# Dilated attention by pairs of heads, with queries and keys stored by class

## The chip, the cores and the metric

The kernel runs on one core of a Trainium2 chip. The time is device microseconds from the first to the last instruction of that core, with what lies around it; the median of the runs counts. Before the change it is 3844.45 us (three runs, 3839.64 to 3844.83).

## What is computed

Two models follow each other on 512 tokens of 1024 features. The first block (two layers: convolution with an mLSTM, then latent attention) is the same before and after the change. The second block has two layers too; each projects the normed tokens to queries, keys and values for two kinds of attention, mixes both by gates, and ends with a feed-forward network. The two kinds:

```python
def differential_attention(q, k, v, lam_full, subln_g, lambda_init):
    ...
        s = jnp.einsum('bqhcd,bkhcd->bhcqk', qblk, kk, ...) * scale
        p = jax.nn.softmax(s, axis=-1)
        a = p[:, :, 0] - lam_full * p[:, :, 1]
        return jnp.einsum('bhqk,bkhe->bqhe', a.astype(v.dtype), v)
...
for g, (window, dilation) in enumerate(((128, 1), (512, 4), (2048, 16))):
    qg = apply_rope(parts[base].reshape(B, S, DB_HEADS, DB_HEAD_DIM), cos, sin)
    kg = apply_rope(parts[base + 1].reshape(...), cos, sin)
    og, lg = dilated_window_attention(qg, kg, vg, dilation, (window // 2) // dilation)
    outs.append(og); lses.append(lg)
wts = jax.nn.softmax(jnp.stack(lses), axis=0)
ob = jnp.einsum('gbsh,gbshd->bshd', wts, jnp.stack(outs))
```

Differential attention has 4 heads of two parts with 64 features each. Dilated attention has 8 heads of 64 features and three groups: a window of 64 tokens to either side; every fourth token; every sixteenth token.

## The kernel before

Tokens are 512 columns, features lie on the 128 rows of a tile, so a tile of queries holds two heads: one on rows 0 to 63, the other on rows 64 to 127. A projection (`fm_g`, lines 365 and 366) adds up 24 products of 128 x 128 by 512 in one of four accumulators `ps_mm`; weights and inputs are in a high and a low part of type fp32r. These products are the "fills": `work()` in `mixer2` yields them a few at a time, and `fill` puts them between the steps of attention by hand-written amounts in us of TensorE (`FILL`, line 1763).

`rope` (line 1518) follows the projection of queries and keys: ScalarE copies the accumulator, four DMAs from ScalarE's queue swap the halves of 32 rows into a tile `rsw` (three buffers), VectorE multiplies by the cosines, GpSimd multiplies the swapped tile by the sines, and VectorE adds both (line 1528).

`diff_unit` (line 1803) makes one head's differential attention for 128 queries: for each of two parts a product over all 128 rows (L1814) and one over the 64 rows of that part (L1815) into one bank `ps_st`, a softmax, transposes (L1835), and the product with the values (L1841). Between the two parts it yields, and fills come in between.

`dil_unit` (line 1863) takes one head `c` of a pair `hp` and one of four classes of tokens (`b`, every fourth token, 128 queries). Its scores are six products for the windows (L1869: 64 rows, 32 columns, 64 to 256 keys) and two for the groups with larger dilation (L1871: 64 rows, 128 columns, 128 keys), all of type fp32 into one bank. Queries and keys are stored in the order of the tokens, so the class is read with a step of four elements:

```python
cv = [a[r0 : r0 + 64].rearrange("p (i b) -> p i b", b=4) for a in t]
...
pe(mm(s[:, P + P * g : 2 * P + P * g], cv[2 * g][:, :, b], cv[2 * g + 1][:, :, b], start=True, stop=True))
```

A softmax on VectorE and ScalarE follows, four transposes (L1885), a copy to `pT` (L1886), and after all eight units of a pair the products with the values (L1898 and L1905), which alternate between the two heads, that is, between output rows 0 to 63 and 64 to 127. Four banks `ps_st` and four buffers `p` serve both kinds of units.

`attend` (line 1767) runs the units by steps: scores of the next unit, fill, transposes of an earlier one, fill, products with the values. `ahead` says how many units are scored before the first is transposed (1 for differential, 2 for dilated units). `mark` and `LAG` let a fill overtake the attention by so many steps at most. What the source orders so is only the order of tracing: a scheduler moves instructions on each engine by its own estimate of times within these bounds, so the order that is built is shown below where it matters.

In the first block one tile `con` holds all constants, loaded by one DMA ahead of the first weights (line 580).

Of the kernel before, what the change touches and what calls it, by code (L numbers as in the profile page):

```python
# [19 lines left out]
P = 128  # L20
D = 1024
KD = 8
# [13 lines left out]
# ---------------------------------------------------------------- parameters  # L36
# [15 lines left out]
_off = 0  # L52
for _n, _w in (
    ("I", 128), ("J", 128), ("NI", 128), ("NJ", 128), ("sel", 8), ("mF", 128), ("mB", 128),
    ("mcos", 64), ("msin", 64),
):
    _CON[_n] = (_off, _w)
    _off += _w
NCON = _off


def _consts():
    con = np.zeros((P, NCON), np.float32)

    def put(n, a):
        o, w = _CON[n]
        con[:, o : o + w] = a
# [34 lines left out]
# windows of 128 keys by first token; the first one goes on from the end at the start  # L102
# [32 lines left out]
def host(inputs):  # L135
# [37 lines left out]
    a["con"] = _consts()  # L173
# [57 lines left out]
# ---------------------------------------------------------------- the program  # L231
class Prog:
# [8 lines left out]
    # -- small helpers  # L241
# [4 lines left out]
    def con(self, n):  # L246
        o, w = _CON[n]
        return self.con_t[:, o : o + w]
# [32 lines left out]
    def weights(self, src, n=WC, lo=None):  # L281
        """A chunk of weights: its two parts, which add up to it."""
# [10 lines left out]
    def split_g(self, hi, lo, src, scale=None, bias=None):  # L293
        """The high part; the function returned makes the low one."""
# [39 lines left out]
    def mm3(self, out, a, b, first, last):  # L334
        """out += a.T b; a and b are (high, low)."""
# [5 lines left out]
    def pe(self, ins):  # L341
        """Other work traced after this does not overtake it by more than LAG stages."""
# [25 lines left out]
    def fm_g(self, wts, rhs, segs, m=P, tag="mm", every=0):  # L368
        """Features on partitions. wts: one (hi, lo, column) per K tile; segs: token ranges. Yields every so many K tiles."""
# [32 lines left out]
    def tm(self, lhss, wts, n, tags=("mm",) * 2 + ("ml",) * 3 + ("st",)):  # L402
        """Tokens on partitions, one output per entry of lhss: (hi, lo) per K tile; wts: (hi, lo, column) per K tile."""
# [11 lines left out]
    def rstd(self, blocks, dim, eps, name, more=None):  # L415
        """(mean + eps) ** -0.5 by token on partitions; blocks, and more to be added to them: [128 features, 128 tokens]."""
# [22 lines left out]
    def over(self, cols, out, mat="I"):  # L439
        """out[:, tokens]: a column by token on partitions, over all partitions along tokens."""  # L440
# [6 lines left out]
    def add_sq(self, S, k, src, a, tile):  # L447
        """Squares of one of the KD tiles, added up in S: [sum, the last ones]; a: the first token."""
# [15 lines left out]
    def factor(self, S, a, b):  # L464
        """The norm's factor for tokens a .. b, over all partitions."""
# [24 lines left out]
    def ada_first(self, d, pool, mp):  # L490
        """Shift and scale of one tile for the first norm."""
# [22 lines left out]
    def ada(self, layer, ch):  # L514
        """Columns 512 ch .. 512 ch + 2047 of the modulation of one layer, into mod[layer], in 16 steps. The four blocks of columns come one below the other."""
# [33 lines left out]
    def fill(self, us):  # L549
        """Steps of other work, for so long on the tensor engine."""  # L550
# [14 lines left out]
    def side(self, n=1):  # L565
        """The next steps of the modulation that is still to be made, between other work."""
# [6 lines left out]
    def first(self):  # L573
        """The first norm, h = rms(x) * (1 + scale) + shift, in two parts, and the first products, as far as the modulation has come."""
# [3 lines left out]
        with tc.tile_pool(name="n0", bufs=2) as tp, tc.tile_pool(name="raw0", bufs=self.RAW0) as rp:  # L578
            self.load_x()
            nc.sync.dma_start(self.con_t, I["con"])  # L580
# [44 lines left out]
    def turn(self, layer, s, hs, acc, tile):  # L625
        """For a norm by parts of the tokens, which follows the updates of x."""
# [9 lines left out]
    def turn_loop(self, st, R, a, b):  # L636
        """h = rms(x) * (1 + scale) + shift, in two parts, for some tokens."""
# [15 lines left out]
    def staged(self, srcs, rhs, ctx=False, tag="mm"):  # L653
        """Features on partitions for up to three chunks of weights, the first part of the tokens first."""
# [25 lines left out]
    # -- layer 0: conformer and mLSTM  # L680
    SEG = [(TC, TA), (0, TC)]

    def mixer0(self, hs, made):
        nc, tc, I = self.nc, self.tc, self.I
        SEG = self.SEG
        with tc.tile_pool(name="m0a", bufs=1) as mp, tc.tile_pool(name="m0t", bufs=2) as tp:
# [3 lines left out]

            cw = mp.tile([P, 4 * CONVW], F32, name="cw")
# [3 lines left out]
            # the gates first: theirs is a long chain  # L695
# [87 lines left out]
    def conv_g(self, mp, j, hs, cw, made=None):  # L783
        """Depthwise over tokens; both ranges in one padded row: y[o] is centred on column o + 15."""
# [40 lines left out]
    def conv_norm(self, mp, accs, mix):  # L825
        """Layer norm and silu of the convolution's output, in two parts."""
# [56 lines left out]
    def gates0(self, mp, tp, G16):  # L883
        """Per direction, by token on partitions: g = log i - cumulative log f, its running maximum G, exp(-m)."""
# [25 lines left out]
        # features on partitions, in the order of each direction's scan  # L910
# [892 lines left out]
    def diff_unit(self, ap, h, qb, qk, va, lam, of, sub):  # L1803
# [6 lines left out]
        for c in range(2):  # L1810
# [11 lines left out]
            if c == 0:  # L1822
                yield
# [287 lines left out]
```

## Time and profile before

| | |
|---|---|
| median of three runs | 3844.45 us |
| lowest, highest | 3839.64, 3844.83 us |
| span of the profiled execution | 3842.6 us |
| TensorE busy | 3718.7 us, 97% |
| weight loads | 3036.5 us, 79% |
| VectorE busy | 2183.8 us, 57% |
| ScalarE busy | 1437.0 us, 37% |
| GpSimd busy | 541.1 us, 14% |

The profile is of one execution. TensorE is in order, and its matmuls overlap: the time that a product costs is read from the start of one to the start of the next in the timeline, not from its duration. A product of type fp32 stands as two records; a projection's product has one. "Waits" are the idle times of an engine, put down to what ended them.

### The profile page before, as it was taken

Reading aid. Unit: us, or ns where it says so; the run is one execution under the profiler, and the core shown is the slowest. Engines: PE = TensorE matmul, PEld = TensorE weight load, DVE = VectorE, ACT = ScalarE, POOL = GpSimd, SP = SyncE. Lnnn points to the kernel's source line nnn. Section 1 sums busy time; section 2 is a strip of 40 time slices with the busy share of each in tenths; the row PEclk is TensorE's granted clock in tenths of the full one; section 3 lists DMA queues with packets and bytes.
Section 4 is the critical chain, followed back from the end, with each engine's and each line's share of the span. In section 5 each row is a group of like instructions: output and inputs, shape, how many; then the busy total and the mean of one; then the engine's idle time right before and its main releaser. Section 6 shows DMA issues by size and latency. Waiting matters only on the chain. (4 is left out here: it accounts for less than half of the span.)

```text
span 3842.6 us, 50218 instructions
## 1 busy us (share of the span) xinstructions
PE 3718.7 (97%) x19848; PEld 3036.5 (79%) x19848; DVE 2183.8 (57%) x3583; ACT 1437.0 (37%) x2507; POOL 541.1 (14%) x528
## 2 busy tenths in 40 slices
PE   7889999999999999999999999999999999999998
PEld 5667877888876767888888778888887887888887
DVE  6976554444447676655665544545567555445545
ACT  4334332222236555333453333432235433333222
POOL 3540100000024211000311200300031111021001
PEclk9989999999999999999999999999999999999999
DMA  5123223332110011332333322223323332222332
GB/s 200 61 91 127 88 91 121 115 110 66 61 51 30 27 34 54 100 98 95 114 90 98 93 64 83 83 90 102 99 81 113 99 90 76 63 95 84 94 98 77
DMA packets 107245, 336.88 MB, mean 88 GB/s; under 512 B 14849, under 2 KB 19457, under 8 KB 106753
## 3 DMA queue, kind: packets, MB, share of 16 engines
q1 hardware_dynamic: 94720, 316.88, 25.7%
q10 hardware_dynamic: 12288, 16.79, 1.7%
q8 instruction: 156, 2.56, 0.3%
q14 instruction: 81, 0.66, 0.1%
HBM read 310.54 MB, written 2.10 MB: 81 GB/s over the span
## 5 line engine op out<-in xcount | busy, mean ns | idle before, releaser
L286 ACT CAST whi<-raw 128x1024 fp32r<-128x1024 f32 (+2 forms) x488 | 501.8, 1031 | 1146.0 <-PE ps_mm L366 702.4
L287 DVE TENSOR_TENSOR wlo<-raw,whi 128x1024 fp32r<-128x1024 f32 (+2 forms) x488 | 616.4, 1265 | 384.0 <-ACT whi L286 381.0
L366 PE MATMUL ps_mm<-h,whi 128*128 128x512 f32 (+2 forms) x2593 | 643.4, 355 | 20.7 <-ACT cth L794 10.3
L366 PE MATMUL ps_mm<-xg,whi 128*128 128x512 f32 (+1 forms) x1929 | 571.7, 378 | 8.2 <-DVE xg L301 6.8
L366 PEld LDWEIGHTS ps_mm<-h,whi 128*128 128x128 f32 (+1 forms) x2593 | 429.1, 189 | 109.2 <-issue 17.3
L366 PE MATMUL ps_mm<-hid,whi 128*128 128x512 f32 (+1 forms) x1805 | 469.5, 357 | 0.0
L366 PEld LDWEIGHTS ps_mm<-xg,whi 128*128 128x128 f32 x1929 | 357.0, 189 | 79.3 <-DVE xg L301 11.2
L366 PE MATMUL ps_mm<-h,wlo 128*128 128x512 f32 (+2 forms) x1298 | 394.9, 354 | 0.5 <-DVE wlo L287 0.5
L365 PE MATMUL ps_mm<-xg,whi 128*128 128x512 f32 (+1 forms) x1207 | 377.3, 392 | 2.8 <-DVE xg L301 2.8
L366 PE MATMUL ps_mm<-xg,wlo 128*128 128x512 f32 (+1 forms) x966 | 362.4, 378 | 0.5 <-DVE wlo L287 0.5
L366 PEld LDWEIGHTS ps_mm<-hid,whi 128*128 128x128 f32 x1805 | 310.2, 188 | 59.4 <-issue 6.7
L366 PE MATMUL ps_mm<-hid,wlo 128*128 128x512 f32 (+1 forms) x903 | 299.0, 356 | 0.0
L365 PEld LDWEIGHTS ps_mm<-xg,whi 128*128 128x128 f32 x1207 | 216.0, 190 | 52.7 <-issue 13.1
L366 PEld LDWEIGHTS ps_mm<-h,wlo 128*128 128x128 f32 (+1 forms) x1298 | 217.9, 189 | 36.2 <-DVE wlo L287 1.0
L365 PE MATMUL ps_mm<-xg,wlo 128*128 128x512 f32 (+1 forms) x602 | 228.9, 383 | 0.0
L366 PEld LDWEIGHTS ps_mm<-xg,wlo 128*128 128x128 f32 x966 | 182.6, 189 | 33.8 <-DVE wlo L287 1.0
L366 PEld LDWEIGHTS ps_mm<-hid,wlo 128*128 128x128 f32 x903 | 160.4, 188 | 24.8
L1527 POOL TENSOR_TENSOR rsw<-rsw,rope 128x512 f32<-128x512 f32 x64 | 105.9, 1656 | 482.1 <-DMA rsw<-qk 439.9
L1153 DVE SCALAR_TENSOR_TENSOR xl<-ps_mm,mod,xl 128x512 f32<-128x512 f32 (+1 forms) x102 | 73.0, 718 | 108.5 <-PE ps_mm L366 108.0
L365 PEld LDWEIGHTS ps_mm<-xg,wlo 128*128 128x128 f32 x602 | 113.8, 189 | 23.1 <-issue 1.4
L365 PE MATMUL ps_mm<-whi,xg 128*128 128x512 f32 x384 | 131.8, 413 | 0.0
L818 DVE SCALAR_TENSOR_TENSOR acc<-up,cw,acc 128x783 f32<-128x783 f32 x80 | 122.7, 1534 | 2.2
(569 smaller groups left out, 5973.0 us busy)
## 6 DMA issues: line engine op xcount, KB each, us to landing
raw<-in_fup SPq DMA_DIRECT2D x88, 512.0 KB, 3.5
raw<-in_sup SPq DMA_DIRECT2D x88, 512.0 KB, 3.5
raw<-in_ada SPq DMA_DIRECT2D x80, 512.0 KB, 3.6
raw<-in_l_qk SPq DMA_DIRECT2D x48, 512.0 KB, 3.5
raw<-in_fdn SPq DMA_DIRECT2D x32, 512.0 KB, 3.4
raw<-in_d_v SPq DMA_DIRECT2D x32, 512.0 KB, 3.8
rsw<-qk ACTq DMA_DIRECT2D x256, 64.0 KB, 2.0
raw<-in_d_gt SPq DMA_DIRECT2D x32, 512.0 KB, 3.5
```

Source lines behind the costliest of these rows:

```text
L286: self.nc.scalar.copy(h[:, :n], r[:, :n])
L287: (lo or self.nc.vector).tensor_tensor(l[:, :n], r[:, :n], h[:, :n].bitcast(F32), ALU.subtract)
L365: return self.nc.tensor.matmul(out, w, x, **k)
L366: return self.nc.tensor.matmul(out, w, x, **k)
L818: nc.vector.scalar_tensor_tensor(acc, u, s, acc, ALU.mult, ALU.add)
L1153: self.pin(nc.vector.scalar_tensor_tensor(xs, o[:, : b - a], self.m(layer, 5, d, int(a < TC)), xs, ALU.mult, ALU.add))
L1527: nc.gpsimd.tensor_tensor(sw, sw, self.SR, ALU.mult)
```

## The change

`dil_unit` now takes both heads of a pair for one class. Each score product of the head on rows 0 to 63 is followed in the source by the same product of the head on rows 64 to 127, into another bank; then two softmaxes, eight transposes. `rope` gets a second form for the dilated queries and keys other than the window's keys: its last addition writes them sorted by class, so that the products read them without a step; its copy of the accumulator then takes an `rsw` buffer (four instead of three). `ahead` is 1 instead of 2 with two heads a unit, and the fills are doubled, so there is as much fill for a head as before. `diff_unit` no longer yields between its two parts: both products over 128 rows, then both over 64 rows. `LAG` is 6 and 4 instead of 8. The constants are in two tiles; the second is loaded when the mixer of the first layer begins. Comments and texts of functions are gone, which moves line numbers.

```diff
-    LAG = (9, 8)
+    LAG = (9, 6, 4)
...
-            self.con_t = cp.tile([P, NCON], F32, name="con")
+            self.con_ts = [cp.tile([P, NCON[0]], F32, name="con"), None]
...
+            self.con_ts[1] = mp.tile([P, NCON[1]], F32, name="con0")
+            nc.sync.dma_start(self.con_ts[1], I["con0"])
...
-    def rope(self, ap, ps):
+    def rope(self, ap, ps, classes=False):
         out = self.tl(ap, [P, T], "qk", bufs=self.QK)
-        nc.scalar.copy(out, ps)
-        sw = self.tl(ap, [P, T], "rsw", bufs=3)
+        raw = self.tl(ap, [P, T], "rsw", bufs=4) if classes else out
+        nc.scalar.copy(raw, ps)
+        sw = self.tl(ap, [P, T], "rsw", bufs=4)
...
+        if classes:
+            o, r, w = (t.rearrange(f, b=4) for t, f in (
+                (out, "p (b i) -> p b i"), (raw, "p (i b) -> p b i"), (sw, "p (i b) -> p b i")
+            ))
+            nc.vector.tensor_tensor(o, r, w, ALU.add)
...
-    FILL = ((1.2, 3.7, 1.2, 1.2), (3.5, 2.2, 1.2), (2, 1.2, 0.7), (4, 12))
+    FILL = ((2.4, 3.7, 1.2), (7, 4.4, 2.4), (4, 2.4, 1.4), (4, 12))
...
-        for c in range(2):
-            s = self.ps("st")
-            s_.append(s)
+        for c, s in enumerate(s_):
+            pe(mm(s, q[:, c, sl], k[:, c], start=True, stop=False))
+        for c, s in enumerate(s_):
             r = slice(64 * c, 64 * c + 64)
-            pe(mm(s, q[:, c, sl], k[:, c], start=True, stop=False))
             pe(mm(s, q[r, c, sl], kl[r], start=False, stop=True))
...
-    def dil_unit(self, ap, hp, c, b, t, vs, dm, of, pTs):
+    def dil_unit(self, ap, hp, b, t, vs, dm, of, pTs):
+        ss = [self.ps("st") for _ in range(2)]
+        rows = [slice(64 * c, 64 * c + 64) for c in range(2)]
+        cls = [a.rearrange("p (b i) -> p b i", b=4)[:, b] for a in t]
         for w in range(4):
...
+                for s, r in zip(ss, rows):
+                    pe(mm(
+                        s[32 * w : 32 * w + 32, c0 : c0 + n], cls[0][r, 32 * w : 32 * w + 32], t[1][r, t0 : t0 + n],
+                        start=True, stop=True,
+                    ))
         for g in (1, 2):
-            pe(mm(s[:, P + P * g : 2 * P + P * g], cv[2 * g][:, :, b], cv[2 * g + 1][:, :, b], start=True, stop=True))
+            for s, r in zip(ss, rows):
+                pe(mm(s[:, P + P * g : 2 * P + P * g], cls[2 * g][r], cls[2 * g + 1][r], start=True, stop=True))
```

What the scheduler makes of it on TensorE in the dilated stage. A row is line, operation, output and inputs; `ps_st` with its numbers is one head's bank, `qk` its queries and keys. Before, a head and class stands alone between fills:

```order
L365 MATMUL ps_mm_3381_18216<-xg_2843_15171,wlo_3380_18213 128x512
L1869 MATMUL ps_st_3382_18240<-qk_3218_17290,qk_3208_17225 32x64
L1869 MATMUL ps_st_3382_18240<-qk_3218_17290,qk_3208_17225 32x192
L1869 MATMUL ps_st_3382_18240<-qk_3218_17290,qk_3208_17225 32x256 x2
L1869 MATMUL ps_st_3382_18240<-qk_3218_17290,qk_3208_17225 32x192
L1869 MATMUL ps_st_3382_18240<-qk_3218_17290,qk_3208_17225 32x64
L1871 MATMUL ps_st_3382_18240<-qk_3280_17633,qk_3274_17587 128x128
L1871 MATMUL ps_st_3382_18240<-qk_3292_17715,qk_3286_17674 128x128
L365 MATMUL ps_mm_3381_18216<-xg_2845_15173,whi_3379_18212 128x512
```

After the change, at the best places (16 of the 32 pairs of both layers), the end of a pair's scores with what follows:

```order
L1878 MATMUL ps_st_3300_17715<-qk_3146_16895,qk_3131_16826 32x192
L1878 MATMUL ps_st_3301_17716<-qk_3146_16895,qk_3131_16826 32x192
L1878 MATMUL ps_st_3300_17715<-qk_3146_16895,qk_3131_16826 32x64
L1878 MATMUL ps_st_3301_17716<-qk_3146_16895,qk_3131_16826 32x64
L1884 MATMUL ps_st_3300_17715<-qk_3178_17046,qk_3161_16971 128x128
L1884 MATMUL ps_st_3301_17716<-qk_3178_17046,qk_3161_16971 128x128
L1884 MATMUL ps_st_3300_17715<-qk_3202_17175,qk_3187_17095 128x128
L1884 MATMUL ps_st_3301_17716<-qk_3202_17175,qk_3187_17095 128x128
L1902 MATMUL ps_st_3253_17456<-con_65,p_3258_17482 128x128 x4
L366 MATMUL ps_mm_3313_17767<-xg_2833_15163,whi_3311_17763 128x512
```

There the two heads, banks 3300 and 3301, take turns product by product. Of the other pairs, 6 stand one head behind the other with no fill between them (4 with one class product before the second head's window products and three after, 2 with the heads complete one after the other), 14 heads stand alone between fills, and 6 heads are split in two by the products with the values.

The differential scores on TensorE, third unit of the first head in the second layer, before; the two banks are the two parts:

```order
L1814 MATMUL ps_st_4288_23697<-dm_4237_23454 128x512
L1815 MATMUL ps_st_4288_23697<-qk_4238_23455,dm_4237_23454 128x512
L365 MATMUL ps_mm_4300_23757<-xg_4146_22806,whi_4298_23753 128x512
L365 MATMUL ps_mm_4300_23757<-xg_4147_22807,whi_4298_23753 128x512
L365 MATMUL ps_mm_4300_23757<-xg_4146_22806,wlo_4299_23754 128x512
L1814 MATMUL ps_st_4291_23711<-dm_4237_23454 128x512
L1815 MATMUL ps_st_4291_23711<-qk_4238_23455,dm_4237_23454 128x512
```

and after:

```order
L1823 MATMUL ps_st_4304_23715<-dm_4253_23472 128x512
L1826 MATMUL ps_st_4304_23715<-qk_4254_23473,dm_4253_23472 128x512
L366 MATMUL ps_mm_4316_23775<-xg_4158_22820,whi_4314_23771 128x512
L366 MATMUL ps_mm_4316_23775<-xg_4159_22821,whi_4314_23771 128x512
L366 MATMUL ps_mm_4316_23775<-xg_4158_22820,wlo_4315_23772 128x512
L366 MATMUL ps_mm_4316_23775<-xg_4160_22822,whi_4314_23771 128x512
L366 MATMUL ps_mm_4316_23775<-xg_4161_22823,whi_4314_23771 128x512
L366 MATMUL ps_mm_4316_23775<-xg_4160_22822,wlo_4315_23772 128x512
L1823 MATMUL ps_st_4305_23716<-dm_4253_23472 128x512
L1826 MATMUL ps_st_4305_23716<-qk_4254_23473,dm_4253_23472 128x512
```

The two parts still stand apart, each with its product over 128 rows and then its product over 64, with six fills between them instead of three. Of the 64 such pairs of products 56 stand alone so after the change; before it there were 54.

## Rows read from the trace of the kernel before

**Rows 1.** Page: busy us of the engines, share of the span, instructions.

```profile
PE 3718.7 (97%) x19848; PEld 3036.5 (79%) x19848; DVE 2183.8 (57%) x3583; ACT 1437.0 (37%) x2507; POOL 541.1 (14%) x528
```

**Rows 2.** Stretches: PE, PEld, DVE, ACT, POOL busy us, clock, DMA share, GB/s.

```profile
2060.00:2312.00 252.00, 250.03 (x1549) 203.27 (x1550) 127.17 (x254) 89.38 (x167) 31.53 (x19) 0.97 0.26 75
...
2293.40:2312.20 18.80, 16.83 (x134) 13.88 (x132) 8.87 (x23) 9.87 (x19) 0.00 (x0) 0.64 0.10 29
2297.00:2310.00 13.00, 11.03 (x68) 9.07 (x70) 5.60 (x17) 6.22 (x13) 0.00 (x0) 0.50 0.10 38
```

**Rows 3.** TensorE's waits, 2060 to 2312 us: in all, times, longest.

```profile
PE ps_st L1885 <- DVE p L1880: 1.1, 1, 1.1
PE ps_st L1898 <- ACT pT L1886: 0.7, 1, 0.7
PE ps_st L1898 <- DVE ps_st L1891: 0.2, 1, 0.2
```

**Rows 4.** Timeline of TensorE, one head and class: start, length, operation, count.

```profile
2236.66 0.39 PE L365 MATMUL ps_mm<-xg,wlo 128*128 128x512 f32 x1
2236.89 0.39 PE L365 MATMUL ps_mm<-xg,whi 128*128 128x512 f32 x1
2237.21 0.68 PE L1869 MATMUL ps_st<-qk,qk 64*32 64x64 f32 x12
2237.82 1.30 PE L1871 MATMUL ps_st<-qk,qk 64*128 64x128 f32 x4
2239.04 0.50 PE L365 MATMUL ps_mm<-xg,whi 128*128 128x512 f32 x1
```

**Rows 5.** Lines L1871 and L994 (ns, min/median/max), and L994 in the timeline.

```profile
L1871 PE MATMUL ps_st<-qk,qk x256: 402/412/600, 2073.2 to 3297.5; 64*128 64x128 f32 x128
...
L994 PE MATMUL ps_ml<-xl,xl x128: 272/272/417, 249.5 to 411.2; 64*128 64x128 f32 x128
...
347.76 0.71 PE L994 MATMUL ps_ml<-xc,xc 64*128 64x128 f32 x4
348.40 0.50 PE L366 MATMUL ps_mm<-h,whi 128*128 128x512 f32 x1
...
306.68 1.16 PE L994 MATMUL ps_ml<-xc,xc 64*128 64x128 f32 x8
307.77 1.05 PE L524 MATMUL ps_ad<-raw,sc 128*32 128x512 f32 x6
```

**Rows 6.** Timeline of TensorE: two column halves in turn.

```profile
2275.65 2.01 PE L1905 MATMUL ps_st<-pT,v 128*64 128x128 f32 x31
2277.60 0.45 PE L1869 MATMUL ps_st<-qk,qk 64*32 64x64 f32 x4
```

**Rows 7.** Timeline of TensorE: 128 rows, then 64 rows.

```profile
1900.69 0.50 PE L1814 MATMUL ps_st<-dm 128*128 128x512 f32 x1
1901.12 0.50 PE L1815 MATMUL ps_st<-qk,dm 64*128 64x512 f32 x1
```

**Rows 8.** VectorE lines (ns, min/median/max); a rotation's addition and a later copy.

```profile
L1528 DVE TENSOR_TENSOR qk<-qk,rsw x64: 673/684/1762, 1882.1 to 3255.3; 128x512 f32<-128x512 f32 x64
...
L1909 DVE COPY of<-ps_st x8: 1067/1080/1084, 2164.7 to 3309.9; 128x512 f32<-128x512 f32 x8
...
2199.43 0.56 ACT L1521 COPY qk<-ps_mm 128x512 f32<-128x512 f32 x1
...
2199.63 0.69 DVE L1528 TENSOR_TENSOR qk<-qk,rsw 128x512 f32<-128x512 f32 x1 [1.17 <-POOL rsw L1527]
```

**Rows 9.** The start: TensorE, GB/s in 3 us slices, SyncE's queue, a user.

```profile
16.36 1.08 PE L497 MATMUL ps_ad<-raw,sc 128*32 128x256 f32 x8 [16.36 <-DMA raw<-in_ada_first]
...
GB/s 103 295 353 370 384 408 412 408 410 411 410 403 369 264 0 3 5 0 0 0 238 112 16 255 261 0 0 0 5 0 122 388 15 0 64 111 0 224 143 162
...
68.00 0.33 SPq L278 DMA_DIRECT2D raw<-in_ada  x1
...
L920 PE MATMUL ps_st<-con,gt x12: 272/272/273, 78.4 to 79.6; 128*4 128x128 f32 x12
```

More of the change, by code (lines that the diff above doesn't have):

```diff
@@ L51 @@
 _CON = {}
[L52 to L59, printed above, removed]
+for _t, _of in enumerate((
+    (("I", 128), ("sel", 8), ("mcos", 64), ("msin", 64)),
+    (("J", 128), ("NI", 128), ("NJ", 128), ("mF", 128), ("mB", 128)),
+)):
+    _off = 0
+    for _n, _w in _of:
+        _CON[_n] = (_t, _off, _w)
+        _off += _w
+NCON = tuple(sum(_w for _t, _, _w in _CON.values() if _t == i) for i in range(2))
 def _consts():
-    con = np.zeros((P, NCON), np.float32)
+    con = [np.zeros((P, n), np.float32) for n in NCON]
     def put(n, a):
-        o, w = _CON[n]
-        con[:, o : o + w] = a
+        t, o, w = _CON[n]
+        con[t][:, o : o + w] = a
     eye = np.eye(P, dtype=np.float32)
@@ L1572, in rope, with rope_c @@
                 return self.rope(ap, o)
+            def rope_c(o):
+                return self.rope(ap, o, True)
             def gate(o):
@@ L1602, in work @@
                         yield from self.values(ap, l, 3, xg, cls, r, 4, v2)
-                    yield from project(I[f"l_qk{l}"][i], lq[i // 6], rope)
+                    yield from project(I[f"l_qk{l}"][i], lq[i // 6], rope if i % 6 == 1 else rope_c)
                 for d in range(3):
@@ L1624, in units @@
                 for hp in range(4):
+                    self.lag = self.LAG[2]
                     pT = []
-                    for u in range(8):
-                        if u == self.READY:
+                    for b in range(4):
+                        if b == self.READY:
                             self.until(lambda: hp == 3 or len(lq[hp + 1]) == 6)
-                        yield 2, self.FILL[1 + (hp > 0)], self.dil_unit(
-                            ap, hp, u // 4, u % 4, lq[hp], (vw, v1, v2), qk["dm"], of[4 + hp], pT
+                        yield 1, self.FILL[1 + (hp > 0)], self.dil_unit(
+                            ap, hp, b, lq[hp], (vw, v1, v2), qk["dm"], of[4 + hp], pT
                         )
@@ L1641, in mixer2 @@
             ys = [self.tl(ap, [P, T], "v", bufs=12) for _ in range(KD)]
-            S = [self.tl(ap, [P, T], "rsw", bufs=3), None]
+            S = [self.tl(ap, [P, T], "rsw", bufs=4), None]
             def made(o, d, a, b):
@@ L1652, in mixer2 @@
             st = self.pre(
-                f"ffn_pre{l}", self.tl(ap, [P, T], "rsw", bufs=3), lambda: self.tl(ap, [P, T], "p", bufs=4)
+                f"ffn_pre{l}", self.tl(ap, [P, T], "rsw", bufs=4), lambda: self.tl(ap, [P, T], "p", bufs=4)
             )
@@ L1742, in swapped @@
         def swapped(src):
-            sw = self.tl(ap, [P, T], "rsw", bufs=3)
+            sw = self.tl(ap, [P, T], "rsw", bufs=4)
             for c, r in enumerate(halves):
@@ L1790, in attend @@
             stage(u)
-            if len(fill) == 4:
-                self.fill(fill[3])
-                stage(u)
             now.append(u)
@@ new lines, in dil_unit @@
+        ps_ = []
+        for s in ss:
+            p = self.tl(ap, [P, T], "p", bufs=4)
+            mx = self.small([P, 1], "mx")
+            nc.vector.tensor_tensor_reduce(p, s, dm[:, b], 1.0, -3e38, ALU.add, ALU.max, mx)
+            nc.vector.tensor_scalar_mul(mx, mx, -0.125)
+            sm = self.small([P, 1], "sm")
+            nc.scalar.activation(p, p, AF.Exp, bias=mx, scale=0.125, accum_out=sm)
+            rs = self.small([P, 1], "rsm")
+            nc.vector.reciprocal(rs, sm)
+            nc.vector.tensor_scalar_mul(p, p, rs)
+            ps_.append(p)
@@ L1881, in dil_unit @@
         yield
         if b == 0:
-            pTs.append(self.tl(ap, [P, 4, 4, P], "pT"))
-        for j in range(4):
-            pe(nc.tensor.transpose(s[:, j * P : j * P + P], p[:, j * P : j * P + P], ident))
-        nc.scalar.copy(pTs[c][:, :, b, :], s.rearrange("p (k q) -> p k q", k=4))
-        if (c, b) != (1, 3):
+            pTs.extend(self.tl(ap, [P, 4, 4, P], "pT") for _ in range(2))
+        for s, p, pT in zip(ss, ps_, pTs):
+            for j in range(4):
+                pe(nc.tensor.transpose(s[:, j * P : j * P + P], p[:, j * P : j * P + P], ident))
+            nc.scalar.copy(pT[:, :, b, :], s.rearrange("p (k q) -> p k q", k=4))
```

43 lines of the change are left out of this document (14 added, 29 removed).

## The prediction

> **What bounds the kernel now.** I read the page first: TensorE is busy for 3718.7 of 3842.6 us, VectorE and ScalarE for 57% and 37% of that time [rows 1]. Then the table by stretches, for the part of the second block in which dilated attention runs (2060 to 2312 us; the second layer repeats it at 3056 to 3309): TensorE 250 of 252 us at 0.97 of full clock, VectorE 127, ScalarE 89 [rows 2]. Then TensorE's waits in that stretch: 2.0 us in all, the two longest 1.1 and 0.7 us [rows 3]. So the products of the projections ("fills", 0.23 us each) stand there without a gap, and whatever TensorE no longer spends on attention comes off the end, as long as the waits stay small. The question is only what the changed products cost on TensorE.
>
> **The dilated scores now.** The timeline of TensorE shows one head and class [rows 4]: last fill at 2236.89, the six window products (L1869, two records each) from 2237.21, the two class products (L1871, four records) from 2237.82, the next fill at 2239.04. That is 2.15 us where a fill alone takes 0.23 (2236.66 to 2236.89), so 1.92 us of TensorE: 0.32 - 0.23 = 0.09 to enter, 0.61 for the windows, 1.22 for the class products. There are 64 such heads and classes in the two layers, 123 us.
>
> **Class products stored by class.** L1871 reads both its operands with a step of four elements; one record takes 412 ns. L994 in the first block has the same shape (64 rows, 128 columns, 128 moving, fp32), reads without a step, and takes 272 ns [rows 5]. In the timeline four records of L994 last 0.64 us up to the next fill (347.76 to 348.40) and eight last 1.09 us [rows 5], so four more records cost 0.45. Stored by class, L1871 becomes L994's form: 1.22 - 0.64 = 0.58 us less per head and class. If the step were not the reason, this is 0; I take 0.58, since the shapes agree in everything else. The Trainium skill (SBUF — State Buffer, Door 1: The DMA port swizzle) says that SBUF is read in lines of 16 bytes and that each access to a new line pays; by that the 16-byte step is the reason here, which these rows bear out.
>
> **Two heads at a time.** Heads of a pair lie on rows 0 to 63 and 64 to 127 and write different banks. No row shows products on two row halves next to each other. The nearest is two column halves: the products of the values (L1898, L1905) alternate between columns 0 to 63 and 64 to 127, and 32 records take 1.95 us (2275.65 to 2277.60), 0.061 each [rows 6], while L994's, on one half of the rows, come every 0.11 us (four in 0.45) [rows 5]. So halves run side by side there. The ends for the second head: nothing, or its full array time, 0.43 us for windows (256 columns in each of four column groups, four times 0.11) and 0.45 for class products. I take nothing, as rows 6 are nearest in kind. The Trainium skill (TensorE: Matmul & The Clock Gate, Part 3: Packing small matmuls) gives 3.07 for four row tiles instead of 4; an estimate by that page has two halves at about 1.5 instead of 2, so 0.25 us more for each pair, about 4 us in all.
>
> **What the built order makes of it.** Only part of the source's order survives. Of the 32 pairs in both layers, 16 stand interleaved (12 window products head by head in turn, then 4 class products); 6 pairs stand one head behind the other without a fill between (4 as six, one, six, three; 2 as six, two, six, two); 14 heads stand alone between fills as before; 6 heads are even split in two pieces by the products of the values. Costs with the rows above:
> - 16 interleaved: before 2 x 1.92 = 3.84; after 0.32 + 0.61 + 0.64 - 0.23 = 1.34; saves 2.50 each, 40.0 us. If the halves take turns instead: 1.34 + 0.43 + 0.45 = 2.22, saves 1.62, 25.9 us.
> - 6 in sequence: 2 x 0.58 and part of one way in and out; between 1.16 and 1.5, I take 1.3: 7.8 us.
> - 14 alone: 0.58 each, 8.1 us.
> - 6 split: 0.58 less one more change of shape, 0.3: 1.8 us.
>
> Sum 57.7 us, or 43.6 if the halves take turns.
>
> **Differential scores.** A product with all 128 rows followed by one with 64 starts 0.43 us later instead of 0.23 (1900.69 to 1901.12), so a change of row count costs 0.20 [rows 7]. The source puts both whole-row products ahead of both half-row ones, but the order built does it at 2 of 32 units and one piece of a third; 56 of 64 products still stand as one pair between other work. Gain: two to three changes of 0.20 and two hidden products, under 1 us; I take 0.6. Had the order followed the source, 32 units would have saved some 0.6 each.
>
> **What the edits cost elsewhere.** Keys and queries stored by class: the last addition of the rotation now reads both operands with the step (40 of 64). It takes 684 ns now [rows 8]; the nearest stepped VectorE row is L1909 with 1080 ns, so 0 to 1.5 us each, 60 us at most over both layers, on an engine idle for 125 us of each such stretch [rows 2]: nothing on the path. The rotation now takes two of four "rsw" buffers instead of one of three, so ScalarE's copy waits for the addition of the rotation before last. At the tightest place that addition starts at 2199.63, after the next but one copy (2199.43) [rows 8]; a wait of about 1 us there is covered by the spare accumulators. The softmax of two heads now follows one scoring: by the order at least 20 fills lie between most scores and their transposes, 5 us or more, as before. I put 2 us for new waits. The stage ends without fills: 18.8 us from 2293.4, of which 13 at half clock (0.50, the 1.2 GHz level) after products of scores and transposes alone [rows 2]. After the change this end has four heads' scores instead of three and 16 transposes instead of 12, but cheaper scores: taken as equal, bounds 3 us longer and 5 us shorter per layer (13 us at the lower level give back 6.5 at most). The constants in two parts: 320 KB less before the first weights, which TensorE awaits until 16.36 us [rows 9]; at the 410 GB/s that the transfers there reach [rows 9], 0.8 us. The second part is issued behind the first products; SyncE's next transfer there starts at 68.00 and the first user at 78.4 [rows 9], so it is hidden. The first block's order changes in many small places; 0, bounds 4 us either way.
>
> Sum: 57.7 + 0.6 - 2 = 56.3 us. The profiled execution spans 3842.6 us, 1.85 below the median of 3844.45. 3842.6 - 56.3 + 1.85 = **3788.2 us**, I say 3788.
>
> **The rivals.**
> - Halves take turns. For: no row shows row halves side by side. Against: column halves [rows 6]. 43.6 + 0.6 - 2 = 42.2: 3802.
> - The step is not the reason for L1871's price. Then lone heads gain nothing, 16 pairs gain 3.84 - (0.32 + 0.61 + 1.22 - 0.23) = 1.92: 31 us, 3814.
> - Every change between the row halves costs what a change of row count costs. An interleaved pair has 15 such changes, the four mixed pairs 4 each: 256 in all. With turns taken and 0.20 us each [rows 7]: 43.6 - 51.2 = -7.6 us, 3852, slower by 0.2%. It decides from 0.17 us a change; below, the kernel is still faster. Against it: the column halves change every 0.06 us without it [rows 6]. The Trainium skill (TensorEngine Tiling (Array Packing), Key Properties) has a change of tiling mode drain the array but not a change of tile; by that rule this rival falls.
> - ScalarE, which works in order, stands at the rotation's copies: a wait that reaches TensorE at each of 40 rotations would have to be 1.4 us to eat the 56 us; 1 us leaves 3828. Against: 5 to 8 us between most copies, and other accumulators to fill.
>
> **How the numbers follow.** The forecast 0.62 (3774 to 3797), halves in turn 0.20 (3795 to 3812), the step 0.06, changes of half 0.07, rotations 0.05. The range from 3772 (ends shorter by 5 us in each layer, start 4 earlier) to 3812 holds the first two, 0.82, which is the 8 in 10. About 0.2%, 7.7 us, is what a measurement of this kernel tells from no change. Faster: 0.62 + 0.20 + 0.06 and half of the rotations, 0.90. Changes of half split between same and slower, with the rest of the rotations: same 0.05, slower 0.05.
>
> **What would show it.** Right: class products at about 270 ns a record; an interleaved pair 1.5 to 1.6 us from the last fill to the next; lone heads 1.57 instead of 2.15; TensorE's waits in the stretch under 5 us; the stretch some 27 us shorter in each layer; differential rows unchanged. Halves in turn: a pair takes 2.4 us. Changes of half: a pair takes over 4 us. The step: records still 412 ns. Wrong altogether: TensorE waiting for ScalarE or VectorE in the dilated stretch for tens of us, or the first 500 us longer by more than the bounds.

## The result and the profile after

The median falls from 3844.45 to 3776.86 us; a fourth run of the kernel before, 6024.52 us, fell in a slow state of the chip and is left out. The ratio over all other runs is 0.9834 (95% interval 0.982 to 0.9847). That is 67.6 us by the medians and 63.8 by the ratio, where 56.3 were forecast, and 3776.86 is inside the range of 3772 to 3812. The profiled executions say the same: spans of 3842.6 and 3773.4 us, 69.2 apart.

The page of the changed kernel shows TensorE as the bound as before (line as in [rows 1]):

```profile
PE 3643.6 (97%) x19848; PEld 2979.0 (79%) x19848; DVE 2191.9 (58%) x3583; ACT 1430.5 (38%) x2507; POOL 543.4 (14%) x528
```

The same 19848 products take 75.1 us less of TensorE; the other engines hardly change. Of the stretches, columns as in [rows 2], the first is the dilated stage, the second its end, in which no fills are left:

```profile
2076.00:2283.00 207.00, 204.75 (x1516) 168.81 (x1515) 121.13 (x241) 84.93 (x161) 29.20 (x18) 0.99 0.30 87
2267.00:2282.60 15.60, 13.35 (x154) 10.94 (x153) 9.81 (x27) 10.95 (x22) 0.00 (x0) 0.89 0.12 35
```

From the first product of the scores to the end of the last product with the values, the stage took 239.7 and 239.8 us in the two layers; now it takes 206.6 and 207.4, although 601 fills lie in it instead of 582. TensorE's waits in the first layer's stage (as [rows 3]):

```profile
PE ps_st L1902 <- DVE p L1895: 1.8, 2, 1.1
PE ps_st L1915 <- DVE ps_st L1908: 0.5, 1, 0.5
```

They sum to 2.3 us, where [rows 3] had 2.0 (1.8 and 2.0 in the second layer): no new wait has come in this stage. In the stretches of differential attention ahead of it TensorE waits 4.3 and 1.4 us in the two layers, where it waited 0.3 and 0.5 before. The longest of these waits is for a softmax on VectorE:

```profile
PE ps_st L1845 <- DVE p L1838: 3.3, 1, 3.3
```

What made the stage shorter is seen in the timeline of TensorE. First a head that stands alone, then an interleaved pair (columns as in [rows 4]; L366 are the fills, L1878 the windows, L1884 the class products):

```profile
2126.52 0.39 PE L366 MATMUL ps_mm<-xg,wlo 128*128 128x512 f32 x1
2126.84 0.65 PE L1878 MATMUL ps_st<-qk,qk 64*32 64x64 f32 x12
2127.41 0.71 PE L1884 MATMUL ps_st<-qk,qk 64*128 64x128 f32 x4
2128.05 0.50 PE L366 MATMUL ps_mm<-xg,whi 128*128 128x512 f32 x1
...
2145.28 0.39 PE L366 MATMUL ps_mm<-xg,wlo 128*128 128x512 f32 x1
2145.60 0.68 PE L1878 MATMUL ps_st<-qk,qk 64*32 64x64 f32 x24
2146.21 0.72 PE L1884 MATMUL ps_st<-qk,qk 64*128 64x128 f32 x8
2146.85 0.73 PE L366 MATMUL ps_mm<-xg,whi 128*128 128x512 f32 x2
```

From the last fill to the next, one head takes 1.53 us (2126.52 to 2128.05; 2.15 in [rows 4]). Two heads take 1.57 (2145.28 to 2146.85), with twice the records. All 14 interleaved pairs between two fills lie within 1 ns of 1.574. One record of the class products is down from 412 [rows 5] to 272 ns:

```profile
L1884 PE MATMUL ps_st<-qk,qk x256: 272/272/374, 2076.6 to 3230.4; 64*128 64x128 f32 x128
```

**Where the gain sits.** I add up, over both layers, the time from the start of each product of dilated attention to the start of the next product on TensorE, and put with the scores what their first product waits beyond a fill's 0.23 us:

| us, both layers | before | after |
|---|---|---|
| scores (windows, class products, way in) | 125.3 | 64.7 |
| transposes | 30.9 | 33.5 |
| products with the values | 39.4 | 30.3 |
| all | 195.6 | 128.6 |

That is 67.0 of the 69.2 us. The other 2.2 are the balance of all the rest, the fills and the 3360 us around the stages, and can't be told from scatter: the order of TensorE's products in the first block is the same in the changed kernel and in all experiments but e7, yet the first differential product starts at times as far apart as these (line of the changed kernel, then of e4; the first start is the number before "to"):

```profile
L1823 PE MATMUL ps_st<-dm x32: 387/397/504, 1899.4 to 2981.4; 128*128 128x512 f32 x32
```

```profile
L1823 PE MATMUL ps_st<-dm x32: 388/397/504, 1906.5 to 2997.9; 128*128 128x512 f32 x32
```

e8 starts it at 1895.8. So some 5 us either way, outside the stage that an edit touches, mean nothing here.

### The profile page after: what moved, and what is told of

Same layout as the page of the kernel before. It is cut to its first block, busy times and chain, and to the rows that moved or that the text cites. A ratio compares the mean times of both kernels' runs of the same rounds, so it can differ in the third digit from the quotient of the medians.

```text
span 3773.4 us, 50278 instructions
## 1 busy us (share of the span) xinstructions
PE 3643.6 (97%) x19848; PEld 2979.0 (79%) x19848; DVE 2191.9 (58%) x3583; ACT 1430.5 (38%) x2507; POOL 543.4 (14%) x528
## 5 line engine op out<-in xcount | busy, mean ns | idle before, releaser
L366 PE MATMUL ps_mm<-xg,whi 128*128 128x512 f32 (+1 forms) x1207 | 373.9, 388 | 2.7 <-DVE xg L302 2.7
L366 PEld LDWEIGHTS ps_mm<-xg,whi 128*128 128x128 f32 x1207 | 219.9, 189 | 49.3 <-issue 5.3
L367 PEld LDWEIGHTS ps_mm<-h,wlo 128*128 128x128 f32 (+1 forms) x1298 | 217.4, 189 | 36.2 <-DVE wlo L288 1.0
L366 PE MATMUL ps_mm<-xg,wlo 128*128 128x512 f32 (+1 forms) x602 | 228.4, 382 | 0.0
L366 PE MATMUL ps_mm<-whi,xg 128*128 128x512 f32 x384 | 132.0, 414 | 0.0
L366 PEld LDWEIGHTS ps_mm<-xg,wlo 128*128 128x128 f32 x602 | 113.8, 189 | 22.2 <-issue 0.7
```

The lines of the kernel that those rows point to most:

```text
L366: return self.nc.tensor.matmul(out, w, x, **k)
L367: return self.nc.tensor.matmul(out, w, x, **k)
```

## The experiments

Theory: storage by class makes each class product cheaper, the two row halves run side by side, both on TensorE, and no other engine becomes late. The rivals are those of the prediction. All medians have four runs; beside them the kernel before had medians of 3845 to 3849 us, so ratios compare best: 0.001 of the ratio is 3.8 us. Each experiment is built anew by the scheduler, so the order on TensorE can change with it; where that bears on the reading, it is said.

| | us | ratio (95%) |
|---|---|---|
| changed kernel | 3776.9 | 0.9834 (0.982 to 0.9847) |
| e1 one head a unit | 3807.3 | 0.9895 (0.9881 to 0.991) |
| e2 step kept | 3807.7 | 0.990 (0.9885 to 0.9915) |
| e3 head after head | 3806.8 | 0.9903 (0.9888 to 0.9918) |
| e4 all pairs interleaved | 3785.1 | 0.9837 (0.982 to 0.9853) |
| e5 differential scores undone | 3781.7 | 0.9827 (0.9812 to 0.9842) |
| e6 differential scores queued | 3783.6 | 0.9833 (0.9817 to 0.9848) |
| e7 one tile of constants, three swaps | 3805.3 | 0.989 (0.9875 to 0.9905) |
| e8 fills later | 3777.2 | 0.9819 (0.9801 to 0.9838) |
| e9 three swap buffers | 3806.2 | 0.9894 (0.9879 to 0.991) |
| e10 five swap buffers | 3783.2 | 0.983 (0.9812 to 0.9849) |
| e11 queued, five swap buffers | 3783.8 | 0.9835 (0.9817 to 0.9853) |
| e12 queued, no stand | 3761.6 | 0.978 (0.9764 to 0.9796) |

**e1: one head a unit.**

```
-    yield 1, FILL, dil_unit(ap, hp, b, ...)            # two heads
+    yield 2, FILL of before, dil_unit(ap, hp, u // 4, u % 4, ...)
```

> The changed kernel with one head a unit again (fills as before the change), storage by class, the regrouped differential scores and the split constants kept. Theory (storage and pairs save separately, on TensorE): all 64 heads stand alone at 1.30 us each, 83 us and some 2 more at half clock, where the changed kernel spends 64.7 us on its dilated scores: +20 us, and the last stretch without fills is again as long as before the change, +3 us in each layer: 3803 us (3798 to 3808). Class products 270 ns a record. Rival, the gain is the storage alone: 3777. Rival, the gain is the pairs alone: 3842 to 3845.

3807.3 us. The lag, and the point by which the next pair must be projected, are those of before as well. All 64 heads now stand alone, at 1.53 to 1.54 us from fill to fill, and the scores come to 84.3 us, where 83 and some 2 were expected. Storage by class without pairs, with the fourth swap buffer that it came with, brings 38.5 us, in the dilated products 195.6 - 149.9 = 45.7. One part of the theory fails: the last stretch without fills takes 16.1 and 15.0 us, not 3 us more than in the changed kernel (15.6 and 16.5).

**e2: the step kept, the pairs kept.**

```
-    project(l_qk[i], lq[i // 6], rope if i % 6 == 1 else rope_c)
+    project(l_qk[i], lq[i // 6], rope)
-    cls = [a.rearrange("p (b i) -> p b i", b=4)[:, b] for a in t]
+    cls = [a.rearrange("p (i b) -> p b i", b=4)[:, b] for a in t]
```

> The changed kernel with queries and keys in the order of the tokens again, so that the class is read with a step of four elements; pairs kept (16 of 32 interleaved in the built order, the other heads in sequence or alone). Theory (a stepped read costs the record, and two row halves run side by side with or without a step): 412 ns a record, an interleaved pair 0.58 us dearer (2.15 us from last fill to next fill), each of the other 32 heads too: 48 x 0.58 = 28 us: 3805 us (3800 to 3810). Rival, stepped reads of two row halves take turns: the eight records of a pair take 2.44 instead of 0.64 us, 16 x 1.8 + 32 x 0.58 = 47 us: 3824. Rival, the step is not what cost: 3777.

3807.7 us. The records are at 412 ns again, and an interleaved pair shows that stepped reads of two row halves run side by side as well (timeline of TensorE, then the class products' durations):

```profile
2148.67 0.39 PE L366 MATMUL ps_mm<-xg,wlo 128*128 128x512 f32 x1
2148.99 0.72 PE L1878 MATMUL ps_st<-qk,qk 64*32 64x64 f32 x24
2149.64 1.30 PE L1884 MATMUL ps_st<-qk,qk 64*128 64x128 f32 x8
2150.87 0.73 PE L366 MATMUL ps_mm<-xg,whi 128*128 128x512 f32 x2
```

```profile
L1884 PE MATMUL ps_st<-qk,qk x256: 406/412/598, 2076.1 to 3264.8; 64*128 64x128 f32 x128
```

Eight class records take 1.23 us (2149.64 to 2150.87), what four took in [rows 4]; the whole pair takes 2.20 (2.15 expected). So the step costs half as much again, and a pair pays it once. Storage alone brings 45.7 us of the dilated products and pairs alone 36.6, but both together 67.0: the parts overlap.

**e3: head after head.**

```
-    for w in range(4):  ...  for s, r in zip(ss, rows): product
+    for s, r in zip(ss, rows):  for w in range(4):  ...  product
```

> The changed kernel with the scores of a pair written head after head; 20 pairs then stand one head behind the other without a fill between, none interleaved. Theory (two row halves run side by side only where they alternate): such a pair takes 2.53 us from last fill to next fill instead of 1.57, for the 16 pairs that are interleaved now 16 x 0.96 = 15 us: 3792 us (3788 to 3797). Rival, the pair saves by one way in and out for two heads, not by running side by side: 1.57 kept, 3777.

3806.8 us. Nothing is left of the pair: the scores take 84.6 us, as with one head a unit. A pair in sequence, in the timeline of TensorE:

```profile
2095.10 0.40 PE L366 MATMUL ps_mm<-whi,xg 128*128 128x512 f32 x1
2095.43 0.65 PE L1878 MATMUL ps_st<-qk,qk 64*32 64x64 f32 x12
2096.01 0.71 PE L1883 MATMUL ps_st<-qk,qk 64*128 64x128 f32 x4
2096.65 0.65 PE L1878 MATMUL ps_st<-qk,qk 64*32 64x64 f32 x12
2097.22 0.71 PE L1883 MATMUL ps_st<-qk,qk 64*128 64x128 f32 x4
2097.86 0.63 PE L366 MATMUL ps_mm<-whi,xg 128*128 128x512 f32 x1
```

It takes 2.76 us (2.75 in most places), not 2.53; I had taken a fill's 0.23 off twice. The halves run side by side only where they alternate. The time lies outside the expected 3788 to 3797 as well: the dilated products lose 20.5 us instead of 15, and another 11 of the 31.5 between the profiled spans lie outside them and stay unexplained, part of them scatter.

**e4: all pairs interleaved.**

```
-    pe(mm(s[...], cls[0][r, ...], t[1][r, ...]))
+    pe(keep_in_program_order(mm(s[...], cls[0][r, ...], t[1][r, ...])))   # all but a unit's first
```

> The changed kernel with each score product of a pair queued behind the one traced before it, so that the built order interleaves all 32 pairs instead of 16 (in 14 of them the first product stands alone ahead of some fills, since the second bank comes free later). Theory: 32 x 1.34 + 14 x 0.25 = 46 us instead of the 64.7 us that the changed kernel spends on its dilated scores: 3759 us (3755 to 3764). Rival, the queued products make TensorE wait for the second bank: the gain comes back as waits, 3777 or slower.

The rival: 3785.1 us, the ratio of the changed kernel. The profiled execution is the slowest of the four, 3800.5 us, so its waits may be longer than those of the median. The score products themselves fall to 46.3 us, but the way in grows from 2.5 to 13.3 us, and transposes and products with the values take 13.5 more. TensorE's waits in the first layer's stage:

```profile
PE ps_st L1910 <- DVE p L1903: 4.4, 3, 2.1
PE ps_st L1886 <- DVE of L1934: 2.7, 2, 2.5
PE ps_st L1886 <- ACT pT L1911: 2.4, 3, 1.9
PE ps_st L1923 <- DVE ps_st L1916: 1.0, 2, 0.6
```

10.5 us where the changed kernel has 2.3. 5.1 of them are waits for a bank at a pair's first score product (L1886): the banks come free too late for two heads at once. Most of the others are waits of the transposes for the softmax.

**e5 and e6: the differential scores,** undone (`diff_unit`, its fills and lag as before), and queued so that the source's order is built:

```
-    for c, s in enumerate(s_):  pe(mm(s, q[:, c, sl], k[:, c], ...))
-    for c, s in enumerate(s_):  pe(mm(s, q[r, c, sl], kl[r], ...))
+    for c in (1, 0):  whole-row product;  for c in (1, 0):  half-row product
+    each but the first: keep_in_program_order
```

> The changed kernel with the differential scores of before the change (each part's two products in a row, a step between the parts, the fills and the lag of before); the rest as changed. Theory (the built order does not regroup, 56 of 64 pairs of products stand alone either way): the two differential stretches and the whole as in the changed kernel, 3777 us (3773 to 3782). Rival, the regroup is part of the 11 us by which the gain is larger than forecast: 3785 to 3790.

> The changed kernel with the four differential score products of a unit queued in the order of the source, so that the built order has both half-row products behind each other in all 32 units of both layers. Theory (a change of row count costs 0.20 us, and the half-row products of the two parts lie on the two row halves and run side by side): each unit saves two changes, 0.40, and one half-row product, 0.2: 32 x 0.6 = 19 us, 3758 us (3753 to 3766). Rival, the queued products make TensorE wait for the second bank: gain under 5 us or a loss, 3772 to 3785.

e5: 3781.7 us, ratio 0.9827: no difference, as was expected of a built order that had not regrouped. e6 has the products cheaper as expected, in the timeline of TensorE (first the changed kernel, L1826 alone, then e6, L1828 of both parts):

```profile
2045.00 0.50 PE L1826 MATMUL ps_st<-qk,of 64*128 64x512 f32 x1
2045.43 0.50 PE L366 MATMUL ps_mm<-xg,wlo 128*128 128x512 f32 x1
```

```profile
1956.31 0.49 PE L1828 MATMUL ps_st<-qk,of 64*128 64x512 f32 x2
1956.73 0.50 PE L366 MATMUL ps_mm<-whi,xg 128*128 128x512 f32 x1
```

Two half-row products take 0.42 us, as one did (0.43). The score products of the two differential stretches take 8.4 and 6.8 us less. Yet the time is 3783.6, no gain, as the rival had it: TensorE's waits in the first such stretch (1904 to 2080) are 10.9 us, 4.3 in the changed kernel:

```profile
PE ps_st L1853 <- ACT pT L1848: 4.9, 2, 4.0
PE ps_st L1847 <- DVE p L1840: 3.9, 2, 2.6
PE ps_mm L367 <- ACT v L1746: 2.1, 1, 2.1
```

and around the longest the granted clock is 0.50 for 6.8 us. VectorE, in the same stretch, stands for DMAs at a rotation's product with the cosines (L1531, in place: it must wait until the swap's DMAs have read the tile):

```profile
DVE rsw L1531 <- DMA rsw<-rsw: 15.1, 5, 4.9
...
DVE qk L1531 <- DMA rsw<-qk: 9.4, 4, 5.7
```

That is 24.5 us, 16.7 in the changed kernel, and the softmax's steps are queued behind it on VectorE. e12 asks whether this is where the gain went.

**e7 and e9: the swap buffers.** The split of the constants leaves 2.5 KB a row free, and the fourth swap buffer takes 2 of them: with one tile of constants only three fit. e7 undoes both, e9 the buffer alone:

```
-    sw = self.tl(ap, [P, T], "rsw", bufs=4)     # all uses
+    sw = self.tl(ap, [P, T], "rsw", bufs=3)
```

> The changed kernel with one tile of constants again, loaded as a whole ahead of the first weights; the 2.5 KB that this takes from each row come from the swap buffers, three instead of four, of which a rotation of a class takes two. Theory (neither bounds): first block within the scatter of the profiles (the first differential product at 1896 to 1906), TensorE's waits for the rotations under 5 us in each layer: 3777 us (3773 to 3784). Rival, ScalarE stands at the rotations' copies with three buffers and TensorE waits for accumulators: 1 us at each of 40 rotations, 3815.

> The changed kernel with three swap buffers instead of four, and the constants left in two parts: the half of the run with one tile of constants that lies in the second block. Theory after that run (a rotation of a class holds two of the swap buffers, and with three the next one's copy on ScalarE and all that is queued behind it there come late): the 28 us of that run come back in full, 3805 us (3798 to 3812), nearly all in the two dilated stretches. Rival, the constants' place cost it: 3777.

3805.3 and 3806.2 us. e7's theory, that neither bounds, was wrong, and e9 puts the loss down to the buffer: it is worth 28 and 29 us by the medians, 22 and 23 by the ratios. The place of the constants is worth nothing that shows. In e9 the dilated stages take 217.4 and 218.2 us, 10.8 longer each. e10 below, whose order in these stages is nearly that of e9, takes 209.2 and 209.6, so the order is not what costs. ScalarE, ahead of the copy that a rotation waits for (lines of L1526: what ended the idle time, us, times), first the changed kernel, then e9; both also stand 10 us there for transfers (DMA rsw<-qk):

```profile
  DVE qk L1537: 0.5, 1
```

```profile
  issue: 14.1, 2
...
  PE ps_st L1884: 9.2, 2
  DMA rsw<-rsw: 6.6, 1
...
  DVE qk L1537: 2.7, 2
```

VectorE stands longer too, at the products with the cosines of a class rotation. Its waits there in the first dilated stage, first in the changed kernel, then in e9:

```profile
DVE rsw L1531 <- DMA rsw<-rsw: 22.4, 11, 4.9
```

```profile
DVE rsw L1531 <- DMA rsw<-rsw: 31.6, 12, 5.0
```

In the timeline (ScalarE, then TensorE) a rotation's copy stands for the last addition of an earlier rotation (L1537), the softmax after it for VectorE (L1892), the transposes' copy follows at 2163.72, and TensorE waits for it:

```profile
2157.62 0.59 ACT L1526 COPY rsw<-ps_mm 128x512 f32<-128x512 f32 x1 [1.45 <-DVE qk L1537]
...
2162.30 0.72 ACT L1892 ACTIVATE p<-p,mx 128x512 f32<-128x512 f32 x1 [4.09 <-DVE mx L1890]
...
2163.72 1.04 ACT L1903 COPY pT<-ps_st 128x512 f32<-128x512 f32 x2
...
2164.82 0.62 PE L1878 MATMUL ps_st<-qk,qk 64*32 64x64 f32 x4 [0.91 <-ACT pT L1903]
2167.11 3.68 PE L1915 MATMUL ps_st<-pT,v 128*64 128x128 f32 x32 [1.66 <-DVE ps_st L1908]
```

The clock falls to 0.50 at 2166 for 6.8 us, and the 32 products L1915 take 3.5 us instead of 1.95. The "issue" of 14.1 us is time that the profile puts to nothing, so how the loss divides between ScalarE's and VectorE's waits stays open.

**e8: fills later.** `FILL` for the later pairs cut from (4, 2.4, 1.4) to (3.6, 2.2, 1.4).

> The changed kernel with the fills of the three later pairs of heads cut from 4, 2.4 and 1.4 us to 3.6, 2.2 and 1.4, so that some are left for the end of the stage: in the built order six fills stand two units of transposes before the end instead of ahead of five units. Interleaved pairs 16 or more as before. Theory (the end of the stage waits for the softmax and drops to half clock for want of fills): the last stretch without fills falls from 15.4 and 16.2 us to about 11, 3768 us (3763 to 3774). Rival, the fills moved are missed earlier and the waits appear there: 3777.

3777.2 us, the rival's number. The end without fills falls from 15.6 and 16.5 us to 14.0 and 13.5, not to 11, and the stages are no shorter than in the changed kernel (206.7 and 209.5). The rival's reason does not show, though: the new wait, 4.2 us in each layer for the softmax of the last pair (L1902), stands in the end itself.

**e10 and e11: five swap buffers,** paid for with one buffer of queries and keys (`bufs=5`, `QK = 10`); e11 has the queue of e6 as well.

> The changed kernel with five swap buffers, paid for with one of the eleven buffers of queries and keys. Theory (with four buffers the rotations no longer hold up TensorE, its waits in the dilated stretch are under 3 us): no gain, 3777 us (3773 to 3782). Rival, four are still short: 10 us or more gained, 3767. If the tenth buffer of queries and keys is what is missed, it is slower, 3785 to 3800.

> The queued differential scores together with five swap buffers and ten of queries and keys. The queued scores alone saved 8.4 us of products in each differential stretch and gave them back, as their trace shows, where VectorE and GpSimd stood at a rotation's swap and TensorE waited behind them. Theory (the swap's transfers are late, not its buffers): a fifth buffer brings nothing back, 3780 us (3776 to 3786). Rival, the buffers are what is late: most of 17 us comes through, 3762 to 3768.

3783.2 and 3783.8 us: paid for in this way, a fifth buffer brings nothing, and does not free e6's gain. What the buffer of queries and keys would have been worth was not separated.

**e12: queued scores, and no stand at the cosines.** To e6's queue is added:

```
-    nc.vector.tensor_tensor(raw, raw, self.CR, ALU.mult)
+    nc.vector.tensor_tensor(o, r, cr, ALU.mult)      # into the class order
     nc.gpsimd.tensor_tensor(sw, sw, self.SR, ALU.mult)
-    nc.vector.tensor_tensor(o, r, w, ALU.add)
+    nc.vector.tensor_tensor(o, o, w, ALU.add)
```

> The queued differential scores, and in the rotations of a class the product with the cosines written straight into the class order instead of in place, so that VectorE no longer waits there until the swap's transfers have read the tile; the addition still waits for the swapped half. Theory (VectorE's stand at that product, 22 us in one dilated stretch of the changed kernel, is what the queued scores' gain was given back to): those waits vanish and most of the 17 us come through, 3762 to 3770 us. Rival, the addition stands for the same transfers, or the gain went elsewhere: 3778 to 3787.

3761.6 us, ratio 0.978, just below the expected range: 84 us below the runs of the kernel before beside it, and faster than the changed kernel. Counted with the fills that moved, the differential stages are 19 us shorter than in the changed kernel, as the expectation of e6 had said, and the dilated ones 5.4 longer (the built order there is another; as many pairs are interleaved). What VectorE stands for in the rotations of a class over the whole program, first in the changed kernel (L1531, then L1537), then in e12 (L1541, the addition; at the product, L1536, it no longer stands for a DMA):

```profile
  DMA rsw<-rsw: 58.8, 32
...
  POOL rsw L1532: 19.2, 17
```

```profile
  POOL rsw L1539: 52.6, 18
```

78.0 us become 52.6 (in e6, to which the edit is added, these rows are 72.1 and 18.6), so the rival is half right too: the addition stands for some of the same transfers. But TensorE's waits in the first differential stretch fall from e6's 10.9 to 4.8 us, all below 2.2, and in the second from 7.7 to 0.8.

That VectorE's stand is the cause is argued, not shown, because the built order changed with the edit. Up to 2031 us of e6 the two orders are the same. Then, where e6 has its longest wait, 9 fills stand between a unit's transposes and its products with the values, and 18 in e12; in the second layer the orders differ throughout. How much each of the two gave was not separated. The out-of-place product without the queue was not tried either, but the gain over the changed kernel lies where the queue saves: the differential score products take 35.2 us over both layers, 53.9 in the changed kernel (4.8 of them waits behind them).

## Why the prediction was right, and where it was off

- **The step:** right. 0.58 us less a head were forecast; 2.152 - 1.534 = 0.62 came, and e1 and e2 show it with and without pairs.
- **Row halves side by side:** right. A pair costs 1.342 us of TensorE beyond a fill, as forecast (1.34), and e3 takes it away by the order alone. With that the rival of halves in turn falls. The Trainium skill (TensorE: Matmul & The Clock Gate, Part 3: Packing small matmuls) measures a gain of 3.07 for four row tiles, from which I had estimated 1.5 for two halves. Here it is 1.94 (two heads alone, 2 x 1.302, by 1.342 for a pair), and the measurement decides. The heads of a pair also write different banks, which no experiment separates from the row halves. But in the kernel before, twelve records of L994 on one row half, four of them into a second bank by the source, take 1.53 us (287.46 to 288.99), 0.11 for each further one as in [rows 5], so a second bank alone saves nothing.
- **Changes of half:** that rival falls by the same pair: 15 changes in those 0.04 us. The Trainium skill (TensorEngine Tiling (Array Packing), Key Properties) has a change of tile drain nothing, and the rows agree.
- **The sum of the scores:** 57.7 forecast, 60.6 measured. The 16 interleaved pairs are as forecast (40.0, from 1.92 a head before); that leaves 20.6 for the other 32 heads instead of 17.7.
- **Waits:** 2 us forecast. In the dilated stages none came (4.1 us over both layers, 4.0 before). In the differential stretches, which the forecast did not look at, they grew from 0.8 to 5.7 us.
- **The end of the stage:** the mis-sized term. I took it as equal with bounds of 3 longer to 5 shorter; it is 3.3 and 2.5 us shorter. The granted clock there is 0.89 instead of 0.64 [rows 2]: the lower level lasts 3.4 us, 6.8 in the second layer, where it lasted 13.7 in both, and in the first layer nearly all of the last products with the values run at full clock:

```profile
2278.73 2.21 PE L1915 MATMUL ps_st<-pT,v 128*64 128x128 f32 x32 [0.49 <-DVE ps_st L1908]
2280.68 2.00 PE L1922 MATMUL ps_st<-pT,v 128*64 128x128 f32 x32
```

  Why the level came back earlier was not tried, and part of it is luck: e6 has the same order of products in the first layer's end and takes 17.5 us there instead of 15.6, and e10, with the same order in both ends, takes 18.0 and 17.5. It is some 6 of the 9.1 us that the products with the values gained, which were in no term; the transposes cost 2.6 more. The dilated products then come to 60.6 + 9.1 - 2.6 = 67.1, the 67.0 of the table. So the forecast was low by the scores (2.9) and by the values less the transposes (6.5), and the 2 us for waits were not needed in this stage.
- **Differential scores:** right that nothing would come (0.6 forecast; e5). For the regrouped order, some 0.6 us a unit, e6 shows 0.47 (8.4 and 6.8 us for 16 units each), and only as a price: there the gain does not come through. In e12, where VectorE stands less at the rotations and the order is another, it does. The forecast took 0.20 us for every change of row count [rows 7], but in the kernel before 30 of the 64 half-row products start 0.32 to 0.33 us after their whole-row product, so only 0.1 is lost there.
- **Rotations:** right for four buffers, and the weak point of the working. I covered a wait at the copies with the spare accumulators and gave their rival 0.05; e9 shows that one buffer fewer costs 22 to 29 us, while ScalarE at the copies and VectorE at the products with the cosines both stand longer. With four buffers the margin was there, but the working did not show it. I had also not seen that the split of the constants pays for that buffer. The last addition takes 1.08 us instead of 0.68 [rows 8] and is hidden, as forecast.

## What to carry to other kernels

Of two products that use half of the rows, the second cost TensorE next to nothing here where it was issued right beside the first and used the other half (0.04 us for the eight products of a head), so interleave them product by product, and read the built order to see that it is so. A gain on the bound engine can be lost again to the engines behind it, when they stand for a transfer with work queued behind: look there, try writing out of place, and count the buffers of the tiles that transfers read. An edit that looks unrelated may be what makes room for that buffer.

## What was not expected of the hardware

- A stepped read costs a half-row fp32 product 412 instead of 272 ns a record, but two on different row halves hide each other's cost: eight records in 1.23 us with the step, as long as four alone (e2).
- In the same order of products, the start of the second block scatters by 10.7 us between profiles (1895.8 to 1906.5): this is the floor for what a change in the first block could show.
